# A hybrid decoder layer on one core: four weight chunks side by side at the start, behind products of zeros

## Chip, cores and metric

The kernel runs on 1 core of a Trainium2 chip. Its time is the device time of one execution in microseconds (us). The program is a list of instructions for five engines that run side by side and wait for each other by semaphores: TensorE (PE: matrix products, with PEld for the loading of stationary tiles), VectorE (DVE), ScalarE (ACT), GpSimd (POOL) and SyncE (SP, which here only issues DMA transfers). ACT and POOL can issue transfers as well.

## What is computed

One decoder layer for 256 tokens of width 2048. Half of the width goes through an RWKV-7 time mixing with 16 heads of 64, the other half through a retention with 4 heads of 256; both read the same input projection. Then follow an output projection, a norm, a squared-ReLU MLP of width 8192 and a second norm.

```python
h = x @ w_in                                   # 2048 -> 7424
y_a = _rwkv7_mix(h[..., :3328], ...)           # r, k, v and three low-rank inputs, with token shift
y_b = _retention_mix(q, k, v, g, ret_gn_w)
mix = jnp.concatenate([y_a, y_b], -1) @ w_o
x = _layer_norm(ALPHA * x + mix, ln1_w, ln1_b)
ff = jnp.square(jax.nn.relu(x @ w_up)) @ w_down
return _layer_norm(ALPHA * x + ff, ln2_w, ln2_b)
```

## The kernel before

**Products.** Every weight is float32. It is split into a high part `hi` (a rounding copy by ACT, line 142) and a rest `lo` (a subtraction by DVE, line 143), and each product is three: hi by the input's high part, hi by its low part, lo by the high part. The weights lie in 202 chunks `ws[i]` of 128 x 2048 floats (1 MB), in the order in which they are used. `prefetch` loads a chunk in two halves into `raw` (three buffers, SP's queue) and splits each half into `whi` and `wlo` (four buffers each, that is two chunks). A chunk of the input projection is 48 products of 256 columns (`stat_tile`, line 159) or 24 of 512 (`mov_chunk`, line 175).

**Start.** The input `xT` (2 MB) and the first two chunks, those of the low-rank inputs, are brought in by hand in four rounds q: a part of x, then a part of chunk 0 and of chunk 1, all on SP's queue, with the split of each right behind (`HEAD_S` says on which engine x is cast). `lora_in` (line 386) multiplies them round by round into two PSUM banks, then `shift` (lines 244 and 245) mixes each with its neighbour token. `ppt`, the table of per-channel parameters, is loaded first on ACT's queue, and six small DVE instructions derive `dp` from it. There are four banks of the kind `mm` and four of the kind `sm`.

**Order.** `large()` is a generator that emits the wide products. After each quarter of a chunk (12 products of 256 columns, or as much) it yields; such a quarter is called a step here. `interleave` then lets the four `rwkv_unit` generators (four heads each) emit a piece of their own work, and each of them says by a `LAG` after how many steps its next piece comes. A unit is taken up when `rwkv_in(u)` starts; it then waits for `("lora", 0)`, for its k, r and v. Its pieces, with the steps between them: the low-rank product (line 552, after 2), the scan (3), the sum of squares (line 585, after 5), the inverse root (1, 1, 1), `bt` and `ar` (7), the grams (line 646, after 2, then 1, 1, 1, 1, 1), 31 dependent substitution steps on DVE (lines 701 and 703) with ten yields of 3 steps, then `bo` (8), then `BGLAG[u]` steps, and then the doubling: `d1` (line 749), `d2` (line 760), which make the inverse of a block of 64 from those of 32. The state updates follow. From the substitution to the doubling the data go through device memory: `blk<-dn`, `dxt<-xb` (line 710) and `xc<-dxt` (line 712), all on SP's queue. While `proj(u + 1)` waits for a buffer of unit u, it yields without a step, so the units catch up.

What is emitted is a priority, not the final order: the framework's scheduler fixes each engine's order when the program is built. It may bring an instruction forward whose inputs are ready; three transfers of unit 0 and of retention (`lupt`, `glupt`, `dmt`), emitted far behind on POOL's queue, are issued at the very start. On the chip each engine works through its own fixed order.

Of the kernel before, what the change touches and what calls it, by code (L numbers as in the profile page):

```python
# [10 lines left out]
F32 = mybir.dt.float32  # L11
# [73 lines left out]
BGLAG = (19, 17, 4, 4)  # L85
# [5 lines left out]
HEAD_S = (0, 1, 0, 1)  # L91
HEAD_PRE = (2, 0)
# [11 lines left out]
def tile_hybrid_layer(ctx, tc, xT, xtok, ws, pp, lup, glup, ln1r, ln2r, cst, rope, dmask, eye, out):  # L104
# [11 lines left out]
    def mm_bank():  # L116
        return ps.tile([P, 512], F32, name="mm", tag="mm", bufs=4)
# [86 lines left out]
    nc.scalar.dma_start(out=ppt, in_=pp)  # L204
# [22 lines left out]
    V.tensor_scalar(out=dp[:, OMU:OMU + 26], in0=ppt[:, MU:MU + 26], scalar1=-1.0, scalar2=1.0,  # L227
                    op0=ALU.mult, op1=ALU.add)
    V.tensor_scalar(out=dp[:, W0H:W0H + 16], in0=ppt[:, W0:W0 + 16], scalar1=0.5, scalar2=None, op0=ALU.mult)
    V.tensor_scalar(out=dp[:, NKK:NKK + 8], in0=ppt[:, KK:KK + 8], scalar1=-1.0, scalar2=None, op0=ALU.mult)  # L230
    V.tensor_scalar(out=dp[:, KAH:KAH + 8], in0=ppt[:, KA:KA + 8], scalar1=0.5, scalar2=None, op0=ALU.mult)
    V.tensor_scalar(out=dp[:, OKA:OKA + 8], in0=ppt[:, KA:KA + 8], scalar1=-0.5, scalar2=1.0,
                    op0=ALU.mult, op1=ALU.add)
    V.tensor_scalar(out=dp[:, RETH:RETH + 8], in0=ppt[:, RETW:RETW + 8], scalar1=0.5, scalar2=None, op0=ALU.mult)
# [41 lines left out]
    with ExitStack() as rctx:  # L276
# [29 lines left out]
        first = [([rp.tile([P, 1024], F32, name="first", tag=t, bufs=n) for t, n in tags],  # L306
                  [(wp.tile([P, 1024], F32R, name="whi", tag="whi", bufs=4),
                    wp.tile([P, 1024], F32R, name="wlo", tag="wlo", bufs=4)) for _ in range(2)])
                 for tags in ((("ar", 2), ("ar", 2)), (("blk", 1), ("vt", 1)))]
        taken[0] = 2  # L310
        for q in range(4):
            raw = rp.tile([P, 1024], F32, name="xraw", tag=("g1", "g2")[q % 2], bufs=2)
            for sl in ((slice(0, 512), slice(512, 1024)) if q == 0 else (slice(0, 1024),)):
                xs = slice(1024 * q + sl.start, 1024 * q + sl.stop)
                nc.sync.dma_start(out=raw[:, sl], in_=xT[:, xs])
                (S.copy if HEAD_S[q] else V.tensor_copy)(xh[:, xs], raw[:, sl])
                V.tensor_tensor(out=xl[:, xs], in0=raw[:, sl], in1=xh[:, xs].bitcast(F32), op=ALU.subtract)
            for i, (raw, parts) in enumerate(first):
                sl = slice(512 * q, 512 * q + 512)
                rw, hi, lo = (t[:, 512 * (q % 2):512 * (q % 2) + 512] for t in (raw[q // 2],) + parts[q // 2])  # L320
                nc.sync.dma_start(out=rw, in_=ws[i][:, sl])
# [55 lines left out]
        def lora_in():  # L377
            lb = [mm_bank(), mm_bank()]
            for q in range(4):
                for i in range(2):  # L380
# [6 lines left out]
                    if (q, i) == HEAD_PRE:  # L387
                        prefetch()
# [799 lines left out]
```

## Time and profile before

| what | us |
|---|---|
| median of 3 runs | 1247.81 |
| lowest and highest run | 1247.39, 1249.36 |
| the profiled execution | 1243.16 |
| its span, first to last instruction | 1241.4 |
| first product | 7.63 |
| mixer with input projection | to about 458 |
| MLP, wide products alone | about 556 to 1230 |

The profiled execution was 4.65 us shorter than the median, so the rows give differences, and a difference is applied to the median. The page is read from the engines' shares to what ends the waits of the busiest one; then the stretch that the change touches is read instruction by instruction. Busy times of PE are modelled ends, so the distance between the starts of two products tells the pace better than the length of one.

### The profile page before, as it was taken

To read this page: it belongs to the slowest core of one execution; us is meant where nothing else is said; L and a number is where in the kernel's file an instruction comes from. 1 tells how busy PE (TensorE), PEld (TensorE's weight loads), DVE (VectorE), ACT (ScalarE), POOL (GpSimd) and SP (SyncE) were. 2 spreads that over 40 slices of the span, in tenths; PEclk is the share of its full clock that TensorE was granted. 3 is DMA by queue.
4 is the path that set the end of the run, shared out by engine and by line. 5 is a ranking of instruction groups with operands and counts; after the bars stand their busy time and mean duration, and the time that the engine had idled before them with its cause. 6 is when DMAs were issued, how large, how long until landed. Compare 5 with 4: busy or idle time off the path is not lost.

```text
span 1241.4 us, 21909 instructions
## 1 busy us (share of the span) xinstructions
PE 1209.7 (97%) x8952; PEld 1089.2 (88%) x8952; DVE 845.8 (68%) x1319; ACT 559.8 (45%) x723; POOL 102.7 (8%) x89
## 2 busy tenths in 40 slices
PE   7999999999999999999999999999999999999996
PEld 7989899879899778779988899988999888999885
DVE  6889998998979656778655555544555545555566
ACT  5545336247434444554443444433454444444341
POOL 0102022001112000008100000000000000000001
PEclk9999999999999999999999999999999999999998
DMA  8674645445454546655755655555555556565562
GB/s 288 200 194 133 175 145 168 133 134 183 138 160 162 181 138 241 211 173 191 268 199 188 206 187 191 186 201 196 194 192 196 186 192 203 189 198 190 193 206 95
DMA packets 86185, 229.76 MB, mean 185 GB/s; under 512 B 30530, under 2 KB 30658, under 8 KB 85316
## 3 DMA queue, kind: packets, MB, share of 16 engines
q1 hardware_dynamic: 83924, 219.38, 54.1%
q0 software_dynamic: 1440, 7.87, 1.8%
q8 instruction: 70, 1.15, 0.4%
q10 hardware_dynamic: 720, 1.11, 0.3%
q14 instruction: 31, 0.25, 0.1%
HBM read 224.59 MB, written 3.74 MB: 184 GB/s over the span
## 4 chain that ended last, share of the span: by engine, by line
PE 85%; DVE 5%; ACT 2%; DMA 2%; issue 1%; POOL 0%; DVEq 0%; SPq 0%; ACTq 0%
PE mm L159 39%; PE mm L175 37%; PE mm L195 4%; DVE wlo L143 1%; DMA raw<-in_ws_dram 1%; PE sm L646 1%; ACT whi L142 1%; PE sm L789 1%; PE sm L781 0%; PE sm L812 0%; DVE wx L143 0%; PE sm L797 0%; PE sm L552 0%; DMA dxt<-xb 0%; PE sm L815 0%
## 5 line engine op out<-in xcount | busy, mean ns | idle before, releaser
L143 DVE TENSOR_TENSOR wlo<-raw,whi 128x1024 fp32r<-128x1024 f32 x372 | 464.8, 1252 | 304.4 <-ACT whi L142 296.9
L142 ACT CAST whi<-raw 128x1024 fp32r<-128x1024 f32 x372 | 391.3, 1052 | 534.1 <-PE mm L175 217.4
L159 PE MATMUL mm<-x1l,whi 128*128 128x256 f32 x928 | 256.2, 276 | 0.0
L159 PE MATMUL mm<-x1h,whi 128*128 128x256 f32 x928 | 256.1, 276 | 0.0
L159 PE MATMUL mm<-x1h,wlo 128*128 128x256 f32 x928 | 256.1, 276 | 0.0
L159 PE MATMUL mm<-xh,whi 128*128 128x256 f32 x640 | 181.4, 284 | 0.0
L159 PE MATMUL mm<-xh,wlo 128*128 128x256 f32 x640 | 177.5, 277 | 0.5 <-DVE wlo L143 0.5
L159 PE MATMUL mm<-xl,whi 128*128 128x256 f32 x640 | 177.4, 277 | 0.0
L175 PE MATMUL mm<-whi,ul 128*128 128x512 f32 x448 | 174.3, 389 | 0.0
L175 PE MATMUL mm<-whi,uh 128*128 128x512 f32 x448 | 174.3, 389 | 0.0
L175 PE MATMUL mm<-wlo,uh 128*128 128x512 f32 x448 | 174.3, 389 | 0.0
L159 PEld LDWEIGHTS mm<-x1h,wlo 128*128 128x128 f32 x928 | 174.2, 188 | 0.0
L159 PEld LDWEIGHTS mm<-x1h,whi 128*128 128x128 f32 x928 | 174.2, 188 | 0.0
L159 PEld LDWEIGHTS mm<-x1l,whi 128*128 128x128 f32 x928 | 174.2, 188 | 0.0
L159 PEld LDWEIGHTS mm<-xh,whi 128*128 128x128 f32 x640 | 120.2, 188 | 3.6 <-issue 1.4
L159 PEld LDWEIGHTS mm<-xh,wlo 128*128 128x128 f32 x640 | 120.3, 188 | 1.0 <-DVE wlo L143 0.7
L159 PEld LDWEIGHTS mm<-xl,whi 128*128 128x128 f32 x640 | 120.4, 188 | 0.3
L175 PEld LDWEIGHTS mm<-wlo,uh 128*128 128x128 f32 x448 | 84.1, 188 | 17.6
L175 PEld LDWEIGHTS mm<-whi,uh 128*128 128x128 f32 x448 | 84.1, 188 | 17.4
L175 PEld LDWEIGHTS mm<-whi,ul 128*128 128x128 f32 x448 | 84.1, 188 | 17.2
L175 PE MATMUL mm<-whi,xh 128*128 128x512 f32 x128 | 52.7, 412 | 0.0
L1078 POOL TENSOR_TENSOR z<-z,lnr 128x512 f32<-128x512 f32 x3 | 3.9, 1291 | 587.0 <-DVE stats L1066 587.0
(272 smaller groups left out, 1608.2 us busy)
## 6 DMA issues: line engine op xcount, KB each, us to landing
raw<-in_ws_dram SPq DMA_DIRECT2D x400, 512.0 KB, 4.4
first<-in_ws_dram SPq DMA_DIRECT2D x8, 256.0 KB, 7.8
z<-in_xtok_dram POOLq DMA_DIRECT2D x2, 1024.0 KB, 10.5
lnr<-in_ln1r_dram POOLq DMA_DIRECT2D x2, 1024.0 KB, 8.5
lnr<-in_ln2r_dram POOLq DMA_DIRECT2D x2, 1024.0 KB, 7.3
xraw<-in_xT_dram SPq DMA_DIRECT2D x3, 512.0 KB, 8.4
dn<-g SPq DMA_DIRECT2D x8, 128.0 KB, 3.2
xc<-dxt SPq DMA_DIRECT2D x8, 128.0 KB, 4.3
```

What stands on the lines that cost most here:

```text
L142: S.copy(hi, raw)
L143: V.tensor_tensor(out=lo, in0=raw, in1=hi.bitcast(F32), op=ALU.subtract)
L159: TE.matmul(dst, w[:, c], a, start=n == 0, stop=n == 3 * KT - 1)
L175: TE.matmul(dsts[tt], a, w[:, c], start=first and k4 == 0 and j == 0, stop=last and k4 == 3 and j == 2)
L195: TE.matmul(dst, a, wt[:, o:o + w], start=kq == 0 and k4 == 0 and i == 0, stop=kq == 3 and k4 == 3 and i == 2)
L646: TE.matmul(bank[r, 128 * n:128 * n + 128], src[r, c64(p, n)], ar[r, o:o + 128], start=True, stop=True)
L789: both(lambda r, p, cp: TE.matmul(sb[r, cp], xt[r, c64(p, n)], rhs[r, cp], start=True, stop=True))
L1078: G.tensor_tensor(out=z[:, tt, cb(n)], in0=z[:, tt, cb(n)], in1=lnr2[:, 0, cb(n)], op=ALU.mult)
```

## The change

- Four chunks instead of two are brought in by hand: to the two low-rank ones come those of unit 0's k. The rounds are six (`HEAD`, first tile of 128 and count): 2, 2, 2, 2, 4 and 4 of the 16 tiles of 128 input channels. Per round a part of x, then that part of each of the four chunks. For the first four rounds the parts of chunks 0 and 2 go on ACT's queue.
- The raw parts and the split parts of the two added chunks lie in tiles that are free at that time (`btok`, `ktok`, `gg`, `mxh` and so on).
- `first_in` replaces `lora_in`: four banks side by side, round by round. It makes k of unit 0 as well, so `rwkv_in(0)` begins with r.
- Ahead of it, `zero` is set by POOL and 18 products of zeros (128 x 128 by 128 columns, float32) are issued into a bank that nobody reads.
- `ppt`, `c1` and the six instructions that derive `dp` come behind the head; the first `lupt`, `glupt` and `dmt` move from POOL's to SP's queue.
- `BGLAG` goes from (19, 17, 4, 4) to (20, 19, 4, 4).

```diff
-BGLAG = (19, 17, 4, 4)
+BGLAG = (20, 19, 4, 4)
-HEAD_S = (0, 1, 0, 1)
-HEAD_PRE = (2, 0)
+HEAD = ((0, 2), (2, 2), (4, 2), (6, 2), (8, 4), (12, 4))
+HEAD_S = (4, 6, 8, 12)
+HEAD_A = 8
+WARM = 18
+HEAD_PRE = (8, 1)
...
-    nc.scalar.dma_start(out=ppt, in_=pp)
...
+        first += [(tiles(512, tags), [(mxh[:, o:o + 1024], mxl[:, o:o + 1024]) for o in (c, c + 1024)])
+                  for c, tags in ((0, ("btok", "ktok", "btok", "ktok")), (2048, ("gg", "bg", "yc", "vtok")))]
+        taken[0] = 4
+        zero = tmp("zero")
+        G.memset(zero, 0.0)
+        idle = sm_bank()
+        for i in range(WARM):
+            TE.matmul(idle[:, 0:P], zero[:, 0:P], zero[:, P:2 * P], start=True, stop=True)
+        for k, n in HEAD:
...
+            nc.sync.dma_start(out=xr, in_=xT[:, xs])
+            (S.copy if k in HEAD_S else V.tensor_copy)(xh[:, xs], xr)
+            V.tensor_tensor(out=xl[:, xs], in0=xr, in1=xh[:, xs].bitcast(F32), op=ALU.subtract)
+            for i, (rws, parts) in enumerate(first):
...
+                (nc.scalar if k < HEAD_A and i % 2 == 0 else nc.sync).dma_start(out=rw, in_=ws[i][:, P * k:P * (k + n)])
                 S.copy(hi, rw)
                 V.tensor_tensor(out=lo, in0=rw, in1=hi.bitcast(F32), op=ALU.subtract)
+        nc.sync.dma_start(out=ppt, in_=pp)
         nc.sync.dma_start(out=c1, in_=cst)
+        derived()
...
         def rwkv_in(u):
             done["start", u] = True
-            yield from proj(u, 8, "k")
+            if u:
+                yield from proj(u, 8, "k")
...
+        def first_in():
+            lb = [mm_bank() for _ in range(4)]
+            for k, n in HEAD:
+                for i in range(4):
+                    hi, lo = first[i][1][k // 8]
+                    for kt in range(k, k + n):
...
+            t = tmp("k")
+            for p in range(2):
+                shift(t[:, hs[p]], lb[2 + p][:, 0:T], 8 + p)
+            done["k", 0] = t
...
-                    nc.gpsimd.dma_start(out=dmt, in_=dmask[:, T * h:T * h + T])
+                    (nc.gpsimd if h else nc.sync).dma_start(out=dmt, in_=dmask[:, T * h:T * h + T])
...
-            nc.gpsimd.dma_start(out=lupt, in_=lup[:, cu])
+            (nc.gpsimd if u else nc.sync).dma_start(out=lupt, in_=lup[:, cu])
...
-            nc.gpsimd.dma_start(out=glupt, in_=glup[:, cu])
+            (nc.gpsimd if u else nc.sync).dma_start(out=glupt, in_=glup[:, cu])
```

## Rows read from the trace of the kernel before

**Rows 1.** The page's span, and its first part: busy us (share) and instructions.

```profile
span 1241.4 us, 21909 instructions
PE 1209.7 (97%) x8952; PEld 1089.2 (88%) x8952; DVE 845.8 (68%) x1319; ACT 559.8 (45%) x723; POOL 102.7 (8%) x89
```

**Rows 2.** PE's waits, whole span: waiter <- releaser: us in total, times, longest.

```profile
PE mm L386 <- ACT whi L322: 8.7, 2, 7.6
PE sm L585 <- ACT hi L581: 3.2, 2, 2.0
PE sm L646 <- DVE bt L631: 1.7, 2, 1.4
```

**Rows 3.** The chain of work that ended last, MLP: start, us, what.

```profile
706.61 87.18 PE mm L159 x768
```

**Rows 4.** Timeline of the start: start, us, engine, line, operation, tiles, shapes [idle before <-releaser].

```profile
0.72 0.86 SPq L315 DMA_DIRECT2D xraw<-in_xT_dram  x2
1.23 0.71 POOL L536 DMA_DIRECT2D lupt<-in_lup_dram  x1 [0.80 <-POOLq L1178]
2.98 0.56 POOL L539 MEMSET zero<- 128x512 f32 x1
...
4.58 0.42 DVE L316 CAST xh<-xraw 128x512 fp32r<-128x512 f32 x1
...
6.96 0.62 ACT L322 CAST whi<-first 128x512 fp32r<-128x512 f32 x1 [4.52 <-DMA first<-in_ws_dram]
...
7.63 0.58 PE L386 MATMUL mm<-xh,whi 128*128 128x256 f32 x1 [7.63 <-ACT whi L322]
...
9.53 0.58 PE L386 MATMUL mm<-xh,whi 128*128 128x256 f32 x1 [1.10 <-ACT whi L322]
...
12.04 0.41 PE L386 MATMUL mm<-xl,whi 128*128 128x256 f32 x1
...
12.26 0.41 PE L386 MATMUL mm<-xh,wlo 128*128 128x256 f32 x1
...
13.75 0.34 PE L386 MATMUL mm<-xh,whi 128*128 128x256 f32 x1
...
14.04 0.28 PE L386 MATMUL mm<-xh,wlo 128*128 128x256 f32 x1
...
14.15 0.28 PE L386 MATMUL mm<-xh,whi 128*128 128x256 f32 x1
```

**Rows 5.** Timeline of PE alone: the first product behind the low-rank chunks.

```profile
22.31 0.28 PE L159 MATMUL mm<-xh,whi 128*128 128x256 f32 x1
```

**Rows 6.** The chain: four PE instructions of float32 products with 128 columns.

```profile
171.07 0.45 PE sm L424 x4
```

**Rows 7.** Busy us by engine, clock, DMA share and GB/s of two stretches.

```profile
5.00:10.00 5.00, 1.27 (x4) 0.97 (x5) 2.91 (x5) 1.24 (x2) 0.00 (x0) 1.00 0.96 319
10.00:15.00 5.00, 5.00 (x30) 5.00 (x30) 3.83 (x6) 3.34 (x5) 0.00 (x0) 1.00 1.04 402
```

**Rows 8.** Timelines of ACT and DVE: the split of a tile of 128 x 256.

```profile
21.52 0.40 ACT L545 CAST lsp<-lupt 128x256 fp32r<-128x256 f32 x1
...
22.06 0.41 DVE L546 TENSOR_TENSOR lsp<-lupt,lsp 128x256 fp32r<-128x256 f32 x1
```

**Rows 9.** Unit 0: its first gram (chain), substitution's end (SP), weights behind it (ACT), doubling.

```profile
60.05 1.09 PE sm L646 x16
...
118.20 0.33 SPq L710 DMA_DIRECT2D dxt<-xb  x1
...
125.81 1.05 ACT L142 CAST whi<-raw 128x1024 fp32r<-128x1024 f32 x1 [7.44 <-DMA raw<-in_ws_dram]
...
L749 PE MATMUL sm<-xc,g x128: 191/191/212, 128.4 to 418.3; 32*32 32x32 f32 x128
```

**Rows 10.** Busy us of PE, PEld, DVE, ACT, POOL in two stretches of the mixer.

```profile
22.00:60.00 38.00, 37.81 (x319) 36.62 (x317) 31.85 (x45) 24.14 (x37) 5.98 (x6) 1.00 0.61 198
...
100.00:133.00 33.00, 32.46 (x317) 31.13 (x315) 30.43 (x59) 15.64 (x24) 6.99 (x6) 1.00 0.50 154
```

More of the change, by code (lines that the diff above doesn't have):

```diff
@@ L226, in tile_hybrid_layer, with derived @@
     OMU, W0H, A0H, NKK, KAH, OKA, RETH = 0, 26, 34, 42, 50, 58, 66
[L227 to L234, printed above, removed]
+    def derived():
+        V.tensor_scalar(out=dp[:, OMU:OMU + 26], in0=ppt[:, MU:MU + 26], scalar1=-1.0, scalar2=1.0,
+                        op0=ALU.mult, op1=ALU.add)
+        V.tensor_scalar(out=dp[:, W0H:W0H + 16], in0=ppt[:, W0:W0 + 16], scalar1=0.5, scalar2=None, op0=ALU.mult)
+        V.tensor_scalar(out=dp[:, NKK:NKK + 8], in0=ppt[:, KK:KK + 8], scalar1=-1.0, scalar2=None, op0=ALU.mult)
+        V.tensor_scalar(out=dp[:, KAH:KAH + 8], in0=ppt[:, KA:KA + 8], scalar1=0.5, scalar2=None, op0=ALU.mult)
+        V.tensor_scalar(out=dp[:, OKA:OKA + 8], in0=ppt[:, KA:KA + 8], scalar1=-0.5, scalar2=1.0,
+                        op0=ALU.mult, op1=ALU.add)
+        V.tensor_scalar(out=dp[:, RETH:RETH + 8], in0=ppt[:, RETW:RETW + 8], scalar1=0.5, scalar2=None, op0=ALU.mult)
     def dcol(base, j):
@@ L303, in diag @@
             return bass.AP(tensor=d.tensor, offset=d.offset + 64 * (m - n), ap=[[2080, 32], [64, n], [1, m]])
[L306 to L321, printed above, removed]
@@ new lines, in tiles @@
+        def tiles(n, tags):
+            return [rp.tile([P, n], F32, name="first", tag=t, bufs=2 if t in TWO else 1) for t in tags]
+        first = [(tiles(1024, tags), [(wp.tile([P, 1024], F32R, name="whi", tag="whi", bufs=4),
+                                       wp.tile([P, 1024], F32R, name="wlo", tag="wlo", bufs=4)) for _ in range(2)])
+                 for tags in (("ar", "ar"), ("blk", "vt"))]
+        first += [(tiles(512, tags), [(mxh[:, o:o + 1024], mxl[:, o:o + 1024]) for o in (c, c + 1024)])
+                  for c, tags in ((0, ("btok", "ktok", "btok", "ktok")), (2048, ("gg", "bg", "yc", "vtok")))]
@@ new lines, in tile_hybrid_layer @@
+        taken[0] = 4
[5 more added lines that the diff above has]
+        for k, n in HEAD:
+            if k % 4 == 0:
+                raw = rp.tile([P, 1024], F32, name="xraw", tag=("g1", "g2")[k // 4 % 2], bufs=2)
+            xr, xs = raw[:, T * (k % 4):T * (k % 4 + n)], slice(T * k, T * (k + n))
+            nc.sync.dma_start(out=xr, in_=xT[:, xs])
+            (S.copy if k in HEAD_S else V.tensor_copy)(xh[:, xs], xr)
+            V.tensor_tensor(out=xl[:, xs], in0=xr, in1=xh[:, xs].bitcast(F32), op=ALU.subtract)
+            for i, (rws, parts) in enumerate(first):
+                g = 16 // len(rws)
+                rw = rws[k // g][:, P * (k % g):P * (k % g + n)]
+                hi, lo = (t[:, P * (k % 8):P * (k % 8 + n)] for t in parts[k // 8])
+                (nc.scalar if k < HEAD_A and i % 2 == 0 else nc.sync).dma_start(out=rw, in_=ws[i][:, P * k:P * (k + n)])
@@ L386, in lora_in @@
                             TE.matmul(lb[i][:, 0:T], w[:, c], a, start=kt == 0 and j == 0, stop=kt == KT - 1 and j == 2)
[L387 removed]
+                    if (k, i) == HEAD_PRE:
                         prefetch()
@@ L508, in large @@
         def large():
-            yield from lora_in()
+            yield from first_in()
             ret = retention()
@@ L535, in rwkv_unit @@
             lupt = rp.tile([P, T], F32, name="lupt", tag="lupt", bufs=1)
-            nc.gpsimd.dma_start(out=lupt, in_=lup[:, cu])
+            (nc.gpsimd if u else nc.sync).dma_start(out=lupt, in_=lup[:, cu])
             if u == 0:
-                zero = tmp("zero")
-                G.memset(zero, 0.0)
                 for dst, src in ((dxt[0:128], zero), (dxt[128:130], zero[0:2]), (xb, eye)):
```

6 lines of the change are left out of this document (removed).

## The prediction

> **What bounds the kernel now.** The page's first part comes first [rows 1]: PE is busy for 1209.7 of 1241.4 us, so a change gains only where PE idles or runs slowly. PE's waits say where it idles by a releaser [rows 2]: 8.7 us before the first products, otherwise at most 3.2 us in total at one place. Then the chain is read at the far end [rows 3]: 768 products of the MLP take 87.18 us without another piece between them, 0.1135 us each. A shift that reaches the MLP therefore comes out whole at the end. So the question is in two parts: how much earlier PE gets through the head, and how much of that reaches the MLP.
>
> The timeline of the head [rows 4] shows two losses. The first product starts at 7.63, because the first weights are only cast at 6.96. Then products of 256 columns start 0.22 us apart (12.04, 12.26), and from 13.75 on 0.11 us apart (14.04, 14.15): these are TensorE's levels of 1.2 and 2.4 GHz. Ahead of the rise PE had worked without a break since 9.53, 4.2 us, and with one break since 7.63, 6.1 us. The 96 products of the two low-rank chunks end at 22.31 [rows 5]; at full pace they need 96 x 0.1135 = 10.9 us. The head costs 22.31 - 10.9 = 11.4 us over its work.
>
> The second bound is DVE in the mixer: from 22 to 60 it is busy for 31.85 of 38 us, from 100 to 133 for 30.43 of 33 [rows 10].
>
> **Products of zeros.** POOL begins its first transfer at 1.23, and sets `zero` in 0.56 us [rows 4]. With the three transfers gone from POOL, `zero` stands at 1.79. A float32 product shows as two PE instructions in the trace (the 8 of line 424 are 16 records); four of 128 columns take 0.45 us [rows 6], 0.1125 each. The 18 products are 36 of them: 4.05 us at the high level, 8.1 at the low one. If the clock rises after 4.2 us of unbroken work, that is at 6.0: 18.7 are done, the other 17.3 take 1.95, and the zeros end at 7.95. If it needs the 6.1 us, the rise is at 7.9, 27 are done and the end is at 8.9. I take the middle, 8.4; a rise that never comes behind them gives 9.9. PE keeps its order, so no real product starts before that.
>
> **Is the data there?** The first part of x was cast at 4.58, behind other work of DVE [rows 4], so it had landed by then. The first round is now 256 KB of x and four times 128 KB, 0.79 MB, half a megabyte behind that x; at the 319 GB/s of 5 to 10 us [rows 7] it is complete by 4.58 + 1.6 = 6.2, and 0.4 more for a cast gives 6.6, under 8.4. Zeros, not data, release PE. After that PE uses up a round of two tiles in 24 products, 2.72 us. A round's transfers take 0.79 MB / 319 GB/s = 2.46 us. ACT casts four parts of 128 x 256 at 0.40 and a part of x at 0.62, 2.2 us; DVE does 4 x 0.41 plus some 0.7 to 1.1 for x, 2.4 to 2.7 us [rows 4, 8]. All three are covered by 2.72, and ACT's eight transfer issues (SP's took 0.43 each [rows 4]) are spent while nothing can be cast yet. The last two rounds move rows twice as long and have more cover. If rows of 1 KB fall below 319 as those fell below the 402 of 10 to 15 us [rows 7], a round takes 0.79 MB / 253 GB/s = 3.1 us, and four rounds cost 4 x 0.4 = 1.6 us. This is the upper bound of this item, zero the lower one; a shorter head than PE's own pace is excluded.
>
> The page "DMA: Bandwidth & Descriptors" of the Trainium skill (Specifications) puts line rate at transfers from 512 bytes up. By it the short rows cost nothing, and a round would take 0.79 MB / 402 GB/s, about 2.0 us; the trace, with 319 GB/s where most rows were 2 KB, does not quite agree, though other things began there too.
>
> **Four chunks side by side.** The number of products is the same: the 96 of unit 0's k move into the head. Both heads compared at the end of k, without the 12 small products of line 552, which both have: before 22.31 + 10.9 = 33.2; after 8.4 + 192 x 0.1135 = 30.2 (29.7 to 30.7). That is 3.0 us (2.5 to 3.5). All four `mm` banks are in use, so r waits for the bank of the first low-rank chunk; that chunk is done 36 products, 4.1 us, before the head's end, against a shift on ACT and one on DVE, under 0.5 us each by the nearest rows [rows 8]. I take 0.2 us off, with 0 and 1 as bounds. Weights of r: their buffers come free as the first halves are used up, 10 us before the head's end.
>
> **Moved behind the head.** `ppt`, `c1` and six small DVE instructions are wanted by the first shift, near 26; DVE is covered. `lupt`, `glupt`, `dmt` join SP's queue, 0.39 MB, 1 us of transfer, wanted after 30 or much later. Nothing, unless SP takes them ahead of weights: then 1 us beneath a supply that is two chunks ahead.
>
> **Unit 0 comes later in the order.** Counting steps from the first product: unit 0 was taken up at 8, waited for k until 16, and its first gram stood behind step 34. Now it is taken up at 16 with k ready; 2+3+5+3+7+2 = 22 and one for the take-up give 39. Five steps are 60 products, 6.8 us; less the 2.8 won, the gram moves from 60.05 to about 64.0 [rows 9]. Unit 1's k ends at step 56 in both, and there unit 0 catches up. The doubling stands `BGLAG` behind: one step (1.36 us) later than before, so at 128.4 - 2.8 + 1.4 = 127.0. The substitution ended at 118.20, and its data took two trips through memory to the doubling, 10.2 us [rows 9]. So gram to doubling had 68.4 us and now has 63.0. For unit 1 the lag of 17 to 19 gives two steps, 2.7 us, of room at no cost, as PE has other products to fill them. The gain is kept whole if unit 0's substitution ends by 127.0 - 10.2 = 116.8, 52.8 us behind its gram instead of 58.1. DVE has the time for it: four splits of k's weights left the stretch, and from 22 to 60 it idled 6.1 us [rows 10].
>
> **The sum.** 3.0 - 0.2 = 2.8 us. On the profiled execution, 1243.16 - 2.8 = 1240.4; it ran 4.65 under the median, so I apply the difference to 1247.81: 1245.0, with 1243.9 to 1245.6 as this case's own range.
>
> **Rivals.**
> - *The substitution is only partly faster.* For: DVE is 92% busy from 100 to 133 [rows 10], and PE already waited there for `bt` [rows 2]. Against: the steps are short and depend on each other rather than on DVE's share. If it ends at 118.2 as before, 1.4 us are lost: 1246.4 (1245.6 to 1247.8).
> - *Slower: the substitution keeps its distance of 58.1 us from the gram.* It ends at 122.2, the doubling can start at 132.4 where 127.0 was meant, and PE or the weights stand: 5.4 - 2.8 = 2.6 us more than before, 1250.4. Splits queued behind the steps on DVE would hold buffers, as ACT once stood 7.44 us for weights [rows 9]. It decides from an end past 119.6 on, where the gain is gone. Against it: the steps are given out together once unit 1's k is done.
> - *The zeros don't raise the clock* (the change doesn't do what it says). Zeros until 9.9, then 4.2 to 6.1 us at half pace cost half of that, 2.1 to 3.0: 12.0 to 12.9 against 11.4, so 1248.4 to 1249.3. Against: for the trace's clock it was enough that PE worked.
> - *The head starves* by 1.6 us: 1246.6.
> - *More than the head*: the looser start of unit 0 also removes waits for `bt` and the sum of squares, 1.7 and 3.2 in total [rows 2], of which 1.5 may be unit 0's: 1243.5.
>
> **How the numbers follow.** 0.2% is 2.5 us, about what a measurement of this kernel can tell from no change: under 1245.3 is faster, over 1250.3 slower. The forecast gets 0.48 (0.42 of it under 1245.3), the partly eaten gain 0.27, the slower rival 0.08 (0.06 over the line), zeros without effect 0.04, starving 0.07, the larger gain 0.06. Faster: 0.42 + 0.06 = 0.48; slower 0.06; same 0.46. The range 1242.6 to 1248.6 leaves out the slower rival, part of the fourth case and the tip of the last.
>
> **What would show it.** In the new profile: zeros from about 1.8, the clock rising at 6.0 to 7.9, first real product near 8.4 with no gap before it; products 0.11 us apart until about 30.2; the first gram near 64, unit 0's last `dxt` by 116.8, the doubling near 127; from the MLP on everything 2.8 us earlier. I am wrong if PE waits in the head, if r waits for a bank, or if the lead of 30 us has shrunk by 134.

## The result: slower by 7.9 us, and the profile of the changed kernel

| | before | after |
|---|---|---|
| median of 6 runs each, us | 1247.6 | 1255.5 |
| lowest and highest | 1246.11, 1249.65 | 1252.56, 1260.37 |
| the profiled execution, us | 1243.16 | 1256.77 |
| its span | 1241.4 | 1255.0 |

The ratio of the times is 1.0061, with an interval of 1.0046 to 1.0076 (the record's ratios are not the quotients of the medians; here and below they differ by up to 0.0013). The forecast of 1245.0 and its range up to 1248.6 were both too low. The profiled execution of before was 4.4 us under its median and that of after 1.3 over, so the spans differ by 13.6 where the medians differ by 7.9.

The page's span and first part, and the first of the MLP's long rows in the chain (columns as in rows 1 and 3):

```profile
span 1255.0 us, 22030 instructions
PE 1224.7 (98%) x8988; PEld 1102.8 (88%) x8988; DVE 846.2 (67%) x1331; ACT 561.3 (45%) x737; POOL 106.6 (8%) x86
...
720.47 87.18 PE mm L165 x768
```

Beside [rows 1] PE is busy for 15.0 us more, DVE for 0.4 more. The 36 records of zeros, 7.1 us, replace idle time; much of the rest is a slower pace, as will be seen. The MLP's 768 products take the same 87.18 us as in [rows 3] and begin 13.86 us later. So everything is lost ahead of them.

PE's waits, whole span (waiter <- releaser: us in total, times, longest):

```profile
PE sm L611 <- ACT hi L607: 4.3, 2, 3.1
PE mm L165 <- DVE wlo L149: 3.2, 1, 3.2
PE sm L972 <- DVE z L964: 2.1, 1, 2.1
PE sm L672 <- DVE bt L657: 1.6, 1, 1.6
PE sm L328 <- POOL zero L325: 1.3, 1, 1.3
PE mm L410 <- ACT mxh L342: 1.1, 1, 1.1
...
PE mm L410 <- DVE wlo L343: 0.7, 1, 0.7
```

The 8.7 us ahead of the first product [rows 2] are gone. L611, L585 before, is the line of a helper that makes two sums, the sum of squares and `bo`; its longest wait rose from 2.0 to 3.1. The tiles tell which sum it is:

```profile
201.95 0.61 ACT L607 CAST hi<-k 128x512 fp32r<-128x512 f32 x1
```

`hi<-k` belongs to `bo`; the sum of squares reads `hi<-sq`. In both kernels the two long waits, near 97 and near 200 us, are for `bo`, of unit 0 and of unit 1, and PE waits at most 0.05 us for a sum of squares. So the prediction's wait for "the sum of squares", and the one for "unit 2's sum" in some expectations below, is the wait for `bo`. New are the wait of 3.2 us for a weight split on DVE, and two in the head (L410).

To see where time goes, the wide products are counted off in steps of twelve in both traces; the table gives the start of a step against the profiled execution of before, in us (minus is earlier).

| step (its start before) | after | e3 | e4 | e12 | e18 |
|---|---|---|---|---|---|
| 4 (16.87) | -3.23 | -1.58 | -2.91 | -4.19 | -3.05 |
| 32 (56.90) | -0.55 | -1.01 | -2.23 | -1.65 | -1.14 |
| 68 (116.73) | -1.43 | -0.57 | -2.74 | -2.36 | -1.24 |
| 76 (131.54) | +2.20 | -0.56 | +1.08 | +0.63 | -1.29 |
| 108 (193.83) | +1.99 | -1.75 | +0.88 | +0.43 | -2.01 |
| 112 (202.75) | +5.79 | -0.14 | +2.03 | +1.44 | +1.97 |
| 188 (350.47) | +6.99 | -0.11 | +3.20 | +2.45 | +3.12 |
| 264 (478.50) | +8.57 | +0.48 | +3.67 | +3.25 | +3.59 |
| 400 (673.81) | +13.86 | +3.78 | +5.23 | +5.15 | +7.35 |

The columns e3 to e18 are experiments, told below. Between steps 264 and 400 all of them fall behind by 1.6 to 5.3, e3 with the old head too: there the profiled execution of before was a short one. Two more experiments, e9 and e10, show how far single executions of one kernel differ: up to 727 us they have the instructions of before, and yet their profiles stand at +1.44 and -0.42 us at step 8, at +4.57 and +0.71 at step 188, at +7.87 and +4.80 at step 400. So the +6.99 of after at step 188 is more than they show, and most of what the change did lies ahead of it. The +2.45 to +3.20 of e4, e12 and e18 are not; for them the runs' times have to decide.

**The head.** Its start (start, us, engine, line, operation; q marks an engine's queue of issues):

```profile
0.72 0.52 POOL L325 MEMSET zero<- 128x512 f32 x1 [0.29 <-POOLq L1204]
...
1.30 7.06 PE L328 MATMUL sm<-zero 128*128 128x128 f32 x36 [1.30 <-POOL zero L325]
...
8.11 0.37 PE L410 MATMUL mm<-xh,whi 128*128 128x256 f32 x1
```

and its ACT, with PE's first wait behind:

```profile
0.72 4.33 ACTq L341 DMA_DIRECT2D first<-in_ws_dram  x5
...
10.06 0.33 ACTq L341 DMA_DIRECT2D first<-in_ws_dram  x1
...
11.20 1.06 ACTq L341 DMA_DIRECT2D first<-in_ws_dram  x2
...
15.84 0.71 ACT L342 CAST mxh<-first 128x256 fp32r<-128x256 f32 x2 [3.73 <-DMA first<-in_ws_dram]
...
16.30 0.39 PE L410 MATMUL mm<-xh,mxh 128*128 128x256 f32 x1 [1.13 <-ACT mxh L342]
```

Zeros from 1.30, 0.21 us apart up to 7.1 and 0.11 from there; the first real product at 8.11, and from the second on 0.11 us between products: as forecast. But ACT issued five of its eight transfers, and the other three only at 10.06 and 11.20, because in its queue they stand behind casts that wait for data. One of those parts landed at 15.84, and PE waited. The lead shrank from 3.23 to 0.55 us.

**118 us.** PE, then DVE ahead of the split that PE wants:

```profile
118.36 0.28 PE L165 MATMUL mm<-xl,whi 128*128 128x256 f32 x1
121.80 0.39 PE L165 MATMUL mm<-xh,wlo 128*128 128x256 f32 x1 [3.17 <-DVE wlo L149]
```

```profile
115.44 0.69 DVE L633 SCALAR_TENSOR_TENSOR t<-t 128x512 f32<-128x512 f32 x1 [0.92 <-POOL t L631]
116.05 0.35 DVE L727 TENSOR_TENSOR prod<-xb,blk 32x200 f32<-32x200 f32 x1
...
119.65 0.67 DVE L640 SCALAR_TENSOR_TENSOR kkr<-y,kkr 128x512 f32<-128x512 f32 x1
120.25 0.36 DVE L729 TENSOR_REDUCE xb<-prod 32x8 f32<-32x216 f32 x1
120.54 1.20 DVE L149 TENSOR_TENSOR wlo<-raw,whi 128x1024 fp32r<-128x1024 f32 x1
```

The split stands behind unit 1's inverse root (L633 to L640), which alternates with unit 0's substitution (L727, L729). PE's row of unit 0's first gram, SP's of its last transfer to memory, and PE's of the doubling:

```profile
66.06 0.43 PE L672 MATMUL sm<-ar,bt 64*64 64x128 f32 x4
...
129.33 0.33 SPq L736 DMA_DIRECT2D dxt<-xb  x1
...
137.23 0.24 PE L775 MATMUL sm<-xc,g 32*32 32x32 f32 x2
```

The substitution, 118.20 before [rows 9], ended at 129.33 and not by 116.8. From the gram to there it is 63.3 us; before it was 58.15 [rows 9], and 52.8 was forecast.

**The clock.** Windows of after (us, busy time of PE, PEld, DVE, ACT, POOL, granted clock, DMA share, GB/s):

```profile
116.00:118.30 2.30, 2.30 (x23) 2.30 (x22) 2.30 (x7) 0.75 (x2) 0.00 (x0) 1.00 0.47 169
118.40:121.80 3.40, 0.23 (x4) 0.04 (x2) 3.40 (x8) 1.00 (x1) 0.00 (x0) 1.00 0.00 0
123.20:126.60 3.40, 3.40 (x18) 3.40 (x17) 3.40 (x7) 0.78 (x2) 0.00 (x0) 0.50 0.87 266
126.60:130.00 3.40, 3.40 (x31) 3.27 (x32) 3.40 (x8) 1.88 (x3) 0.00 (x0) 1.00 0.49 174
...
202.70:208.50 5.80, 5.80 (x25) 5.61 (x26) 5.55 (x8) 2.70 (x4) 2.48 (x3) 0.50 0.33 116
...
549.90:553.20 3.30, 3.22 (x16) 2.79 (x14) 2.57 (x7) 2.12 (x5) 0.00 (x0) 0.50 0.38 134
```

Behind the wait at 118 the granted clock is 0.50, the level of 1.2 GHz, for 3.4 us; behind the one at 199 (3.1 us) for 5.8. PE is "busy" there at half its pace: 1.7 and 2.9 us are lost besides the waits. A third stretch of 3.4 us, at 549.87, follows a wait of 2.4 us for `z` and costs 1.7 more. The profile of before has no such stretch in the middle, though its wait for `z` is nearly as long (2.1 us). The three make 6.3 of the 15.0 us more of busy time, beside the 7.1 of the zeros. That is one execution; over all runs on record the mean granted clock is 0.9930 in the six of after and 0.9959 in those of before beside the experiments. By this difference the low clock makes some 3.6 of the 7.9 us (0.0029 of 1255; an estimate).

### The profile page after: what moved, and what is told of

The parts are those of the page before. It is cut to its first block, busy times and chain, and to the rows that moved or that the text cites. A ratio compares the mean times of both kernels' runs of the same rounds, so it can differ in the third digit from the quotient of the medians.

```text
span 1255.0 us, 22030 instructions
## 1 busy us (share of the span) xinstructions
PE 1224.7 (98%) x8988; PEld 1102.8 (88%) x8988; DVE 846.2 (67%) x1331; ACT 561.3 (45%) x737; POOL 106.6 (8%) x86
## 3 DMA queue, kind: packets, MB, share of 16 engines
q8 instruction: 70, 1.15, 0.4%
## 4 chain that ended last, share of the span: by engine, by line
PE 80%; DVE 9%; ACT 5%; DMA 4%; issue 2%; POOL 0%; SPq 0%; DVEq 0%; ACTq 0%
PE mm L165 35%; PE mm L181 34%; PE mm L201 3%; DMA raw<-in_ws_dram 3%; DVE wlo L149 2%; ACT whi L148 1%; PE sm L672 1%; PE mm L410 1%; DMA first<-in_ws_dram 1%; DVE prod L727 1%; DVE xb L729 1%; DVE wx L149 1%; PE sm L815 1%; ACT sw L703 1%; PE sm L807 0%
## 5 line engine op out<-in xcount | busy, mean ns | idle before, releaser
L149 DVE TENSOR_TENSOR wlo<-raw,whi 128x1024 fp32r<-128x1024 f32 x368 | 459.1, 1250 | 311.2 <-ACT whi L148 305.1
L148 ACT CAST whi<-raw 128x1024 fp32r<-128x1024 f32 x368 | 386.6, 1052 | 514.6 <-PE mm L181 212.0
L165 PE MATMUL mm<-xh,whi 128*128 128x256 f32 x608 | 173.9, 286 | 0.0
L165 PE MATMUL mm<-xh,wlo 128*128 128x256 f32 x608 | 170.3, 280 | 3.2 <-DVE wlo L149 3.2
L165 PE MATMUL mm<-xl,whi 128*128 128x256 f32 x608 | 170.5, 280 | 0.0
L165 PEld LDWEIGHTS mm<-xh,wlo 128*128 128x128 f32 x608 | 116.0, 191 | 3.6 <-DVE wlo L149 3.4
L165 PEld LDWEIGHTS mm<-xh,whi 128*128 128x128 f32 x608 | 115.8, 190 | 3.3 <-issue 0.9
L165 PEld LDWEIGHTS mm<-xl,whi 128*128 128x128 f32 x608 | 115.8, 191 | 0.6 <-issue 0.2
L181 PEld LDWEIGHTS mm<-whi,ul 128*128 128x128 f32 x448 | 84.1, 188 | 17.2
L181 PE MATMUL mm<-whi,xh 128*128 128x512 f32 x128 | 52.8, 413 | 0.0
```

The costliest lines, as they stand in the source:

```text
L148: S.copy(hi, raw)
L149: V.tensor_tensor(out=lo, in0=raw, in1=hi.bitcast(F32), op=ALU.subtract)
L165: TE.matmul(dst, w[:, c], a, start=n == 0, stop=n == 3 * KT - 1)
L181: TE.matmul(dsts[tt], a, w[:, c], start=first and k4 == 0 and j == 0, stop=last and k4 == 3 and j == 2)
```

## Experiments

Times are medians; beside each stands the kernel before in the same runs on the same chip: 1247.55 for e1 to e4, 1248.28 for e5 to e8, 1247.35 for e9 to e12, 1248.13 for e13 to e16, 1247.48 for e17 and e18. Brackets hold the ratio's interval.

### The parts, one by one: e3, e5, e7, e8

e3 is the kernel before with the zeros alone, e5 the changed one without them:

```diff
 e3 (before): + zero = tmp("zero"); G.memset(zero, 0.0); idle = sm_bank()
              + for i in range(18): TE.matmul(idle[:, 0:P], zero[:, 0:P], zero[:, P:2 * P], start=True, stop=True)
              - zero = tmp("zero"); G.memset(zero, 0.0)        # its old place, in unit 0
 e5 (after):  -WARM = 18
              +WARM = 0
```

> The kernel before with the 18 products of zeros alone. If the zeros do what I worked out, the clock is up near 7, the products of the head start near 8 at 0.11 us apart, but two chunks can't fill the head: their data come in until 18 and the last product ends at about 20.5 instead of 22.3. Theory A (only the place of unit 0 matters): everything behind it stands as before, and 1.5 to 2 us of gain reach the end, 1245.5 to 1246. Rival (the stretch from 84 to 133 is set by VectorE, which gains nothing): 1247 to 1248, the same as before.

> The changed kernel without the products of zeros. The clock then rises 4 to 6 us after the first real product, near 10, and the head loses about 2 us of pace; its waits for data near 15 and 18 shrink by as much, since PE comes to them later. Theory A (the place of unit 0 in the order costs the time, the front hardly matters): the same time as the changed kernel within 1.5 us, 1254 to 1257. Rival (the front's gain does reach the end): 2 us and more above it, 1257 to 1259.

e3 took 1245.62, 0.9993 [0.998, 1.0006]: products of zeros win 1.6 us in the head, and nothing is left of it at step 112. At step 108 the lead was still 1.75; then PE waits for unit 1's `bo`, as long as in the profile of before (2.16 and 2.15 us), but in this execution 3.4 us at 1.2 GHz follow and in before's none. e5 took 1254.36, 1.0036 [1.002, 1.0053]; from step 8 on it leads by the same 0.56 us as after does. So in the changed kernel's profile the zeros' gain was lost in the head's waits for data: PE only arrived earlier at the same late data.

e7 and e8 put the other two parts into the kernel before: unit 0's gram five steps later, and the new `BGLAG`.

```diff
 e7 (before): -yield LAG["kk"]
              +yield LAG["kk"] if u else 12
 e8 (before): -BGLAG = (19, 17, 4, 4)
              +BGLAG = (20, 19, 4, 4)
```

> The kernel before with one lag of unit 0 raised from 7 steps to 12, so that its first gram stands behind step 39 as in the changed kernel: the suspected cause by itself. Theory A: unit 0's last dxt transfer comes 5 us or more after 118.2, PE waits 2 to 4 us for a low part of weights near 118 to 122, and the time rises by 3 to 6 us, to 1250.5 to 1253.5. Rival (the cost comes from the new head, its buffers or its transfers): within 1.5 us of before.

> The kernel before with the new lags 20 and 19 alone. If the lags cost by themselves, as the changed kernel with the old ones suggests (5 us less), the wait of the sum near 195 grows to 3 us or more, with the clock falling behind it, and the time rises by 2 to 5 us, 1249.5 to 1252.5. If they only cost where unit 0 is late, it stays within 1.5 us of before.

Both took 1249.03, 1.0012 [0.9998, 1.0026] and 1.0015 [0.9999, 1.003]: 0.8 us each by the medians, and neither can be told from before. In e7 the substitution ended at 133.66, 66.2 us behind its gram (58.15 before): the five steps alone lengthen it. Yet PE, which came to 118 without a lead, waited only 0.7 us for the split there. A late unit 0 alone is not enough.

### Undoing parts of the change: e1, e2, e4, e6

```diff
 e1 (after): -yield LAG["kk"]
             +yield LAG["kk"] if u else 2          # unit 0's gram at step 34, as before
 e2 (after): -BGLAG = (20, 19, 4, 4)
             +BGLAG = (19, 17, 4, 4)
 e4 (after):  for k, n in HEAD:                    # a first loop that only issues
             +    nc.sync.dma_start(out=xr, in_=xT[:, xs])
             +    (nc.scalar if ... else nc.sync).dma_start(out=rw, in_=ws[i][...])
             +for k, n in HEAD:                    # a second that casts and subtracts
 e6: e1, e2 and e4 together
```

> The changed kernel with one lag of unit 0 cut from 7 steps to 2, so that its first gram stands again behind step 34 as before the change (it stood behind 39). Theory A (the five steps by which unit 0 comes later push its substitution into unit 1's work on VectorE): the stall of 3.3 us near 118 shrinks under 1, unit 0's last dxt transfer comes 5 us or more earlier, and the time falls by 3 to 7 us below the changed kernel, to about 1249 to 1252. Theory B (the place of unit 0 doesn't matter; the longer lags of the doubling are what hurts): within 1 us of the changed kernel, or PE now waits for bt at the gram.

> The changed kernel with the old lags 19 and 17 ahead of the doubling. Theory A: the doubling of unit 0 waits for its substitution, which is late, so the time is the same or up to 3 us longer, and the stall near 118 stays. Theory B: the stall of 3.3 us near 199, where unit 0's last pieces meet unit 1's on ScalarE, goes back to the 2.2 us of before, the clock keeps its high level there, and the time falls by 3 to 5 us.

> The changed kernel with all transfers of the head ahead of its casts, so that ScalarE issues its eight in one go at the start (the sixth to eighth came at 10 to 12 us, behind casts that wait for data). If PE's two waits in the head, 1.3 and 0.9 us near 15 and 18, come from these late issues, they go, and the head ends 2 us earlier, near 30.6 instead of 32.8. If the transfers as such are too slow, the waits stay at other places. At the end theory A expects little of it, within 2 us of the changed kernel, as the stall near 118 grows by what was won.

> The changed kernel with the three repairs of the runs before at once: all transfers of the head ahead of its casts, unit 0's first gram behind step 34, the old lags 19 and 17. Each alone took 4 to 5 us off. Theory A: the wait for the weights' low part near 118 is gone by the gram's place, the head ends near 30.6, and the time falls to 1245 to 1248, at or a little under the kernel before; the wait of the sums near 195 stays at 2 us and eats up what is left of the front's gain. Rival (each repair removes the same loss): no better than any one of them, 1250.

| | us | ratio | PE's waits and the clock |
|---|---|---|---|
| e1 | 1250.33 | 1.002 [1.0001, 1.0039] | none at 118; 1.6 at 62 for bt, 2.33 at 198.5, then 1.2 GHz |
| e2 | 1250.15 | 1.0034 [1.0018, 1.0049] | 3.38 at 119 stays, 2.4 GHz behind it; 1.70 for the doubling; 2.03 at 197, then 1.2 GHz |
| e4 | 1251.37 | 1.0039 [1.0019, 1.0059] | none over 0.5 in the head; 3.42 at 117, then 1.2 GHz; 3.31 at 198, 2.4 GHz behind it |
| e6 | 1249.5 | 1.0003 [0.9989, 1.0017] | 0.9 in the head, none at 118; 3.33 at 59.5 for bt, 3.03 at 196, 1.2 GHz behind both |

e4 settles the head: with all transfers ahead of the casts PE leads by 2.7 us from step 8, which is the forecast's own 2.8. But of the 2.15 us that it leads over after at step 8 (-2.70 against -0.55) 1.7 are left at step 32 and 1.1 at step 76. Against the 1255.5 of after each repair brings 4 to 5.4 us by the medians and 2.7 to 5.1 by the ratios, and the three together 6.0 or 7.2. That is a comparison with other runs, and the intervals of e2 and e4 overlap with after's; those of e1 and e6 don't. So the three parts hold the whole loss, while what stays in e6 (the zeros, four chunks side by side, the moved tables) neither costs nor wins anything that could be told at the end. The repairs don't add up: PE, now earlier, waits at the next place where it needs a chain of DVE or ACT. e6 shows it best, with an early head and an early gram: PE waits 3.3 us for unit 0's bt. The wait near 199 falls back to 2.33 us in e1 and 2.03 in e2, but it is 3.03 in e6 with both undone: what sets its length is not shown.

### What a wait costs: e9 and e10

In the MLP of the kernel before, where nothing else disturbs PE, waits are made on purpose.

```diff
+ if i == 0 and sl and len(us) in (1, 3, 5, 7):      # between two tiles of the up product
+     sx = mp2.tile([P, 512], F32, name="sx", tag="rl", bufs=2)
+     V.tensor_copy(sx[:, 0:256], bank[:, 0:256])
+     for _ in range(4):                             # e10: 0
+         V.tensor_copy(sx[:, 0:256], sx[:, 0:256])
+     x0 = x1h[:, 0:256]                             # rewritten with its own value
+     V.scalar_tensor_tensor(out=x0, in0=sx[:, 0:256], scalar=0.0, in1=x0.bitcast(F32), op0=ALU.mult, op1=ALU.add)
```

> The kernel before, with twelve waits made on purpose in the MLP, where PE otherwise works without another piece: behind the first half of every second pair of tiles DVE copies the finished bank (five copies of 128x256 and one weight split of 1.2 us between them) and then rewrites a part of the input with its own value, so that PE's next product waits. By DVE's rows (0.3 to 0.4 us a copy) PE stands 3.3 to 4 us each time. Theory: a wait of this length is followed by a stretch at 1.2 GHz, as in the changed kernel behind 118.36 (3.33 us, then 3.4 us at 1.2 GHz) and 199.23 (3.28, then 6.8). At half pace 3.4 us lose 1.7, so twelve waits cost 12 x (3.6 + 1.7) = 64 us or more, and the products behind each wait stand 0.227 apart. Rival: the low clock has other reasons; then 12 x 3.6 = 43 us, and the products stand 0.113 apart at once.

> The same twelve waits, with one copy and the rewriting instead of five copies: PE stands 1.0 to 1.4 us each time. Theory: waits this short are not followed by a lower clock (the kernel before has waits of 1.1 to 2.2 us and its profile shows 2.4 GHz behind them), so the cost is the waits alone, 12 x 1.2 = 14 us. Rival, that any wait of PE brings the clock down: 12 x (1.2 + 1.7) = 35 us.

Of the twelve places nine made PE wait; at the last of each slice it had products of another kind to go on with. One wait of e9, and its windows:

```profile
756.09 0.28 PE L159 MATMUL mm<-x1h,wlo 128*128 128x256 f32 x1
759.78 0.49 PE L159 MATMUL mm<-x1h,whi 128*128 128x256 f32 x1 [3.41 <-DVE x1h L1039]
760.07 0.42 PE L159 MATMUL mm<-x1l,whi 128*128 128x256 f32 x1
```

```profile
756.40:759.70 3.30, 0.00 (x0) 0.00 (x0) 3.10 (x8) 0.98 (x1) 0.00 (x0) 1.00 0.54 169
759.78:763.20 3.42, 3.42 (x16) 3.42 (x17) 0.00 (x0) 0.00 (x0) 0.00 (x0) 0.51 0.39 146
763.20:766.00 2.80, 2.80 (x26) 2.80 (x25) 0.58 (x1) 1.05 (x1) 0.00 (x0) 0.99 0.00 0
```

and the same of e10:

```profile
751.70:752.80 1.10, 0.08 (x1) 0.00 (x0) 0.94 (x3) 1.04 (x1) 0.00 (x0) 1.00 0.44 127
752.85:756.30 3.45, 3.45 (x30) 3.45 (x31) 1.20 (x1) 0.49 (x1) 0.00 (x0) 1.00 0.65 194
```

In e9 all nine waits are 3.57 us over the usual distance, and eight of them are followed by some 3.4 us with products at twice their distance, 16 of them in a window that held 30 in e10. In e10 the waits are 1.23 us and none is followed by it. e9 took 1296.69, 1.039 [1.0358, 1.0421]; from step 400 to the end its trace falls behind by 47.6 us, 5.3 a wait: 9 x 3.57 + 8 x 1.7 = 45.7, and 1.9 beside. e10 took 1265.54, 1.0135 [1.0104, 1.0165]; 18.2 us in that stretch: 11.1 are the waits, the other 7.1 come in steps of 0.2 a chunk between them and were not followed up. So the clock's share of a wait like the one at 118 is shown: some 1.7 us on top. It isn't sure in every instance: one of e9's nine went without it. Counted over the middle of all profiles (20 to 1230 us, without the waits made in e9 and e10), no wait of 1.0 to 1.8 us was followed by the low clock (75 of them), 16 of the 39 of 1.8 to 2.8 us were, and 14 of the 19 longer ones. So whether a wait of 2 us costs 2 or 3.7 differs from one execution to the next, as before and e3 show at `bo`.

### Order or load on DVE: e11 to e18

```diff
 e12 (after): -yield LAG["rn"]
              +yield LAG["rn"] + (2 if u == 1 else 0)    # unit 1's inverse root two steps later
              -yield LAG["kk"]
              +yield LAG["kk"] - (2 if u == 1 else 0)
 e11: e4 and e12 together, and unit 2's sum four steps later
```

> The changed kernel with one edit: unit 1's inverse root comes two steps later in the order (and the lag behind it two steps shorter), which puts the split of the awaited half chunk ahead of it on DVE. Nothing else. Theory: the wait of 3.33 us at 118.36 stood there because DVE worked off unit 1's root first; it goes, with the low clock behind it: 3.3 + 1.7 = 5 us less, 1250.5. Rival, DVE is short of time in this stretch whatever its order: the wait turns up within 15 us of 118 at another instruction (the sum, bt or the doubling), and the time stays at 1254 to 1256.

> The changed kernel with three repairs: all transfers of the head are issued ahead of the casts (2.2 us in the head, as measured), unit 1's inverse root two steps later and its next lag two steps shorter (so that DVE splits the half chunk that PE waited for at 118 first), and unit 2's sum of squares four steps later (PE waited for it at 199). Theory: PE's lead of 2.5 us at 30 us now lives past 118 and 200, so 1247.6 - 2.5 = 1245.1, down to 1243 if fewer waits bring the clock down. Rival: the lead is eaten at the next place where PE meets a chain of DVE, whichever it is: 1247 to 1249.

e12 took 1250.86, 1.0028 [1.0012, 1.0043]; e11 1250.93, 1.0029 [1.0013, 1.0045]. In e12 the time is close to the 1250.5 of its theory, and the wait of 3.3 us for the split is 0.4; but 2.5 us turn up at 124.2, where unit 1's first gram waits for `bt` and `ar`, as its rival said. Its lag at step 188 is smaller partly because no low clock followed its wait of 3.16 us at 197.8. e11 leads by 3.45 us at step 68, and by nothing at step 76, for the same reason. Whatever the lead, unit 1's `bt` was ready at nearly the same time: 125.58 before, 127.34 after, 126.25 in e4, 125.22 in e11, 125.84 in e12 (and 128.26 in e9, that is in another execution of before). e11's third edit missed its aim: PE's wait of 3.16 us at 197.2 is for unit 1's `bo`, and unit 2's sum of squares comes behind it, at 210.5, where PE waits 0.05 us.

The next runs change DVE's load. e13 to e16 give four splits to POOL, e17 and e18 leave four low parts of weights out (ACT fills them with zeros).

```diff
 e13 (after), e14 (before), e15 (e4), e16 (e4 and e12's edit):
-    V.tensor_tensor(out=lo, in0=raw, in1=hi.bitcast(F32), op=ALU.subtract)
+    (G if (i, h) in ((12, 1), (13, 1), (14, 1), (15, 1)) else V).tensor_tensor(out=lo, ...)
 e17 (after), e18 (e4):
+    if (i, h) in ((13, 1), (14, 1), (15, 1), (16, 1)): S.activation(lo, raw, AF.Copy, scale=0.0)
+    else: V.tensor_tensor(out=lo, ...)
```

> The changed kernel with four weight splits taken from DVE and given to POOL (the second halves of chunks 12 to 15, consumed between 85 and 112 us), nothing else. POOL is busy for under a tenth of the span; by its 1.46 to 2.45 us for a product of 128x512 a split of 128x1024 takes it 2.9 to 4.9 us, against 1.2 on DVE. Theory: DVE is the bound between 30 and 126 us (unit 1's bt ends at 125.2 to 128.2 in every version, whatever PE's lead), so with 4.8 us of its work gone unit 1's bt ends 3 to 5 us earlier, at 123 to 124.5, the wait of 3.3 us at 118 shrinks under 1.5 and the time falls by 3 to 6 us, to 1249.5 to 1252.5. Rival, the order on DVE and not its load sets this point: bt stays at 127 +- 1 and the time at 1254 to 1256. A third: DVE slows down while POOL works beside it, and nothing is won.

> The kernel before with the same four splits on POOL. Theory (DVE is the bound there): unit 1's bt, at 125.58 in the kernel before, ends at 121 to 123, but PE only waited 1.1 to 1.4 us in this stretch, so no more than about 2 us come out: 1245 to 1247.5. Rival (order, not load): bt within 1 us of 125.6 and the time unchanged.

> The changed kernel with all transfers of the head ahead of the casts, and the four splits on POOL. Theory: PE's lead of 2.5 us at 30 us is kept past 126, since DVE can now follow: step 76 of the main work 2 to 2.7 us earlier than in the kernel before, and the time 1245 to 1248 (what is left is the wait at 196 to 200 for unit 2's sum). Rival: the lead is gone at 126 as in the others, 1249.5 to 1251.5.

> As the one before, and unit 1's inverse root two steps later, which put the split that PE waited for at 118 ahead of it on DVE. Theory: with DVE's load lowered the order matters less, so within 1.5 us of the run without it, 1244.5 to 1248. Rival, that the order is what counts: clearly better than that run, by 3 us or more, as the same edit alone brought 4.6 us to the changed kernel.

The third case named for e13 came out, that DVE slows down beside POOL. POOL's split and a small instruction of DVE beside it:

```profile
84.84 0.17 DVE L729 TENSOR_REDUCE xb<-prod 128x4 f32<-128x16 f32 x1
85.02 2.39 POOL L149 TENSOR_TENSOR wlo<-raw,whi 128x1024 fp32r<-128x1024 f32 x1 [4.38 <-ACT whi L148]
85.05 2.41 DVE L727 TENSOR_TENSOR prod<-xb,blk 128x25 f32<-128x25 f32 x1
87.49 0.18 DVE L729 TENSOR_REDUCE xb<-prod 128x5 f32<-128x25 f32 x1
```

A product of 128x25, 0.19 us in after, took 2.41, to the end of POOL's split. So POOL could take away 2.4 us of DVE's time where a split costs DVE 1.2, and these runs don't lower DVE's load as planned. Unit 1's `bt` came later: 130.16 in e13 (127.34 without), 134.06 in e14 (125.58), 130.65 in e15 (126.25), 129.62 in e16. e14 took 1255.63, 1.0072 [1.0047, 1.0097]: the kernel before, with DVE held up, is as slow as the changed one. But PE's long wait is at another place here: 3.5 to 4.2 us in e13, e15 and e16 and 7.1 in e14 for unit 0's `bo` near 96 (1.4 without POOL), in e14 behind a scan that DVE needed 2.66 us for beside POOL's split (0.68 in after). The substitution itself ended 61.3, 56.6, 61.7 and 60.9 us behind its gram, a little sooner than without POOL. So these runs show what holding DVE up costs, and don't separate load from order at 118. e13 took 1254.72, 1.0061; e15 1253.84, 1.0048; e16 1251.48, 1.0024. The 2.4 us between e15 and e16, the edit of e12, lie within their intervals.

> The changed kernel, where four low parts of weights (second halves of chunks 13 to 16, split between 92 and 109 us) are left out: ACT fills them with zeros (1.04 us each by its casts), so VectorE has 4 x 1.21 = 4.8 us less to do and GpSimd is not used. Theory, VectorE's time is the bound up to 126 us: unit 1's bt ends at 122.5 to 124.5 instead of 127.34, the wait at 118 falls under 1.5 us, and the time falls by 3 to 6 us, to 1249 to 1252. Rival, the order on VectorE alone sets it: bt at 127 +- 1 and 1254 to 1256.

> The same four parts left out, with all transfers of the head ahead of the casts. Theory: PE's lead of 2.5 us at 30 us is now kept past 126 (step 76 of the main work 1.5 to 2.7 us earlier than in the kernel before, where the head alone gave +1.1 and 0.0), and the time is 1246 to 1249, with the wait for unit 2's sum near 198 left. Rival: the lead is gone at 126 all the same, 1250 to 1252.

With the load lowered, e17 took 1251.19, 1.0028 [1.0011, 1.0045], and e18 1250.01, 1.0007 [0.9988, 1.0025]. In both the wait at 118 is gone without an edit of the order; but with four instructions fewer the scheduler ordered DVE anew, and in e17 the splits stand between the last instructions of the root, no longer behind them. `bt` came at 126.49 in e17, 0.85 earlier and not the 3 to 5 expected, which is what the rival asked for, while the time is what the theory asked for; PE was 1.5 us behind after's profile at step 32. In e18 it came at 124.33, 1.9 earlier than in e4. What moved most is the substitution:

```profile
117.49 0.33 SPq L746 DMA_DIRECT2D dxt<-xb  x1
```

It ended at 117.49 in e18 and 119.65 in e17, 52.0 and 52.1 us behind its gram instead of 63.9 (e4) and 63.3 (after). Now the lead survives this stretch in a kernel with the new head for the first time: -1.14 at step 32, -1.29 at 76, -2.01 at 108. Then comes unit 1's `bo` (PE and ACT of e18, and its windows behind):

```profile
192.51 0.28 PE L168 MATMUL mm<-xh,whi 128*128 128x256 f32 x1
196.23 0.79 PE L621 MATMUL sm<-hi,ones 128*128 128x512 f32 x1 [3.44 <-ACT hi L617]
```

```profile
195.56 0.61 ACT L617 CAST hi<-k 128x512 fp32r<-128x512 f32 x1
```

```profile
196.70:201.70 5.00, 5.00 (x23) 4.81 (x23) 4.75 (x8) 2.32 (x4) 2.51 (x3) 0.50 0.41 129
```

ACT makes `hi` at 195.56, behind a row of copies, where the kernel before made it at 195.66. PE came 2 us earlier, so its wait was 3.4 us instead of 2.0 [rows 2], and 5 us at 1.2 GHz followed: a lead of 2.0 us became a lag of 2.0.

## Why the prediction was wrong, point by point

- **Zeros and first product.** Right: 1.30 and 8.11 for 1.8 and 8.4, the pace doubling 5.8 us after the first zero where 4.2 to 6.1 were taken. In the profiles of e3 and e4 it doubled after 3.5 and 4.3 us, so that 8.4 came out to 0.3 us is in part luck. The trace of e3 shows that the zeros win 1.6 us in the head by themselves.
- **"Is the data there?"** The first step that failed. Sizes and rates were right: e4 has no wait over 0.5 us in the head and the lead of 2.7 us. Wrong was the half-sentence on issuing, that ACT's eight issues "are spent while nothing can be cast yet". Only five were; the other three took their places behind casts in the same queue. The loss, 2.2 us between after and e4, was above the bound of 1.6 that I gave for slow rows. I had counted issues by their duration and not by what stands ahead of them.
- **The bank for r, the moved tables.** Right: no wait of PE for either appears in the trace.
- **"DVE has the time for it."** The step that decided. The forecast asked for the substitution to end by 116.8, 52.8 us behind a gram at 64.0; the gram came at 66.06, 2 us late by the head's loss, and the end at 129.33, 63.3 us behind it. This distance hardly differs between executions: it is 58.2 to 58.7 in before, e3, e8, e9 and e10, and 62.9 to 63.9 in after, e2, e4, e5, e11 and e12. With nothing but the gram five steps later it is 66.2 (e7), with the gram put back 56.2 and 57.6 (e1, e6). So the five steps, which were to leave it shorter, made it longer. DVE's timelines, counted from the first substitution step to the last transfer, show how:

| DVE's instructions there | before | after | e18 |
|---|---|---|---|
| the stretch, us | 38.7 | 45.2 | 33.6 |
| 62 of the substitution, busy us | 17.2 | 17.1 | 18.3 |
| weight splits | 10, 12.1 us | 12, 14.7 us | 5, 6.1 us |
| others | 22, 12.0 us | 29, 16.7 us | 22, 12.0 us |
| idle us | 1.9 | 2.3 | 0.9 |

Neighbours overlap by some 0.05 us, so that the parts make more than the whole. DVE has no room in this stretch, and the substitution takes as long as what is put between its steps: five steps later, that is more of unit 1's pieces. The 6.1 us of idle DVE that I read as room lie between 22 and 60, ahead of the first step at 79.5. After idles there even more, and it doesn't help (columns as in rows 10):

```profile
22.00:60.00 38.00, 38.00 (x318) 37.01 (x317) 30.81 (x49) 24.42 (x39) 5.82 (x6) 1.00 0.67 227
```

The table also refutes what I held against the partly faster substitution, that the steps "depend on each other rather than on DVE's share". e17 and e18 confirm the load: with four splits out (three more then fall behind its end) the distance is what the forecast had asked for. e12 shows that an edit of DVE's order leaves the distance at 62.9 and moves PE's wait to another instruction.
- **The slower rival** named the right engine and the point from which it decides (an end past 119.6), with a chance of 0.08 and a price of 2.6 us. Even its distance of 58.1 us was too short. The place of the wait was another: not the doubling but the split at 118, where the rival had only spoken of splits that hold buffers, and `bo` at 199. The price was missing the clock.
- **More than the head.** The 1.7 and 3.2 us of [rows 2] are waits for `bt` and for `bo`, not for a sum of squares; unit 0's part of them is 0.24 and 1.21, and no wait for `bt` lies between 100 and 133, where the partly faster rival put one. In after `bt` makes unit 0 wait no longer, but `bo` does, 1.21 as before.
- **The clock behind a wait.** Mis-sized by omission. The sum priced a wait by its length. e9 measured 5.3 us for one of 3.57. The two in after: 3.3 + 1.7 at 118 and 3.3 + 2.9 at 199, 11.2 us. Against them stand before's waits near the same places, 1.15 at 132.8 and 2.15 at 194.1 by the distances of its products, and the lead of 1.43 at step 68: 11.2 - 3.3 - 1.4 = 6.5, of the 7.0 that after's profile lags at step 188 and the 7.9 between the medians.
- **A lead is kept until the MLP.** Wrong in every profile that had one: up to 3.45 us (e11, step 68) were gone by step 112. e3 and e18 kept theirs up to step 108 and lost it at `bo`.

What stays open: no run moved the work for unit 1's `bo` on ACT (e11 delayed another sum), so whether a lead that passed the wait near 196 would reach the MLP wasn't seen. How much of e17 and e18 is DVE's load and how much its new order isn't separated either. The best median, 1245.62 (e3), can't be told from the kernel before.

## What to carry to other kernels

A busy engine with gaps is not freed by sending it ahead: if a second engine is full in some stretch, the first arrives earlier and waits longer there, and a longer wait is more often followed by a low clock, which costs half as much again (e9: 1.7 us on 3.57). Before crediting a lead, look for the next row in which the leading engine waits for another, and ask whether that releaser moves too. Look for an engine's room in the very stretch where the work will run, and count what stands between its steps. And before explaining 2 us by two profiles, see how far two executions of the same kernel differ. Transfers that an engine issues stand in its queue like its other work, so issue them ahead of anything that waits for data.

## What the runs showed of the hardware

- A wait of TensorE of 3.57 us was followed eight times in nine by some 3.4 us at 1.2 GHz; one of 1.23 us never (e9, e10). In the other stretches of all profiles 16 of 39 waits of 1.8 to 2.8 us were followed by it.
- A subtraction of 128x1024 on GpSimd took 2.4 us, and a VectorE instruction with two inputs that began beside it stood until its end (0.19 to 2.41 us, e13). The Trainium skill says so on the page "SBUF — State Buffer" (section "SBUF: two separate sides"): VectorE with two inputs from SBUF and GpSimd take turns at a shared port, for whole instructions. The trace agrees. I had not weighed it before giving GpSimd the splits.
